# A plain first block of the MLP, small parameters as one load, and VectorE's share of the convolutions in a three-layer hybrid kernel

## The chip, the cores and the metric

The kernel runs on one core of a Trainium2 chip. The metric is the device time of one execution in microseconds (us); a lower time is better. Before the change the median of three runs is 1737.26 us (1736.63 to 1739.16).

The core's engines are TensorE (PE in the rows, its weight loads PEld), VectorE (DVE), ScalarE (ACT), GpSimd (POOL) and SyncE (SP), which issues the DMAs. Each works through its own queue in order.

## The reference

Input: x of 512 tokens by 1024, float32. Two layers of a first block and one layer of a second run one after the other.

```python
for l in range(2):                       # first block
    p = x @ w_in[l]
    y_a, y_b, y_c = mla(...), mlstm(...), ssd(...)   # ssd: 5-tap convolution over 768 channels, silu, scan
    x = layernorm(2 ** 0.5 * x + concat(y_a, y_b, y_c) @ w_out[l])
    x = layernorm(2 ** 0.5 * x + moe(x))             # 16 experts, 2 per token
h = rmsnorm(x, norm_mix_w)               # second block
x = x + concat(gated_delta_net(h), rg_lru(h)) @ w_out_2
m = rmsnorm(x, norm_mlp_w)
u = relu(m @ w_ff1)                      # 1024 x 4096
x = x + (u * u) @ w_ff2                  # 4096 x 1024
return rmsnorm(x, final_norm_w)
```

## The kernel before

**Numbers.** Every matrix product of weights and activations is made of three TensorE products: an operand is split into a high part (a cast, line 134) and a low part (the operand less its high part, line 139), and high x high, high x low and low x high are summed (lines 124 to 126). `split` takes the engine of each part: the cast is on ScalarE, the low part on VectorE or GpSimd.

**Weights.** `plan` lists all weights as tasks in the order of their use. `pump` loads a task as soon as the ring of split weights has room: SP issues a DMA into a raw buffer (line 229), then units of 1024 columns are split, the engines taken in turn from `self.pat`. In the mixers `pat` starts as ("act", "dve") and turns to ("act", "pool") behind the projection "C" of the gates (line 520), so from the convolutions on GpSimd makes the low parts. A raw buffer is loaded again when its last split has read it. The order on each engine is laid down by a planner when the kernel is built: it goes by program order and by modelled times, so that an instruction may be pulled ahead of earlier ones of its queue.

**Small parameters.** `params` (line 2007) makes one tile for each of 8, 9 or 6 groups of columns and issues one DMA for each (line 2014). The tiles have one buffer each, so a group for the next layer is loaded when the last reader of that group is done. `params_done` halves the convolution's weights (line 2018).

**The start** (`run`). SP issues four loads of x (already transposed), two of the weights "C", the parameters, then the first convolution weights into the buffers of "C". ScalarE and VectorE split x and weights, the projection "C" runs over four token tiles, and its evacuation (lines 506 to 515) has steps on VectorE and on ScalarE; two PSUM banks take turns.

**The convolutions** (`ssd_conv`, line 580). Three tasks of two features each: 24 matmuls of 512 columns make one feature (128 channels by 512 tokens). The evacuation copies it with padding (ScalarE, line 592), makes the first tap with bias on VectorE (line 594), adds four taps there (line 596), takes tanh (ScalarE, line 598), multiplies (line 600); four of the features are then transposed on TensorE (line 605). Beside this VectorE works through the small steps of the gates (lines 435 to 445 and 700 to 735), and GpSimd, besides weights, through products for the scan (lines 625 and 662).

**The MLP of the second block.** The output projection of the mixer (`out_last`, line 1016) ends tile by tile of 128 tokens; `fin` (line 1884) normalizes each tile, and `mlp_in` transposes it (line 1770) and splits it. The up projection works in 8 blocks of 512 columns. Each block is a 2 x 2 product (two halves of the 1024 features, two halves of tokens, two halves of columns) done by a scheme with 7 products instead of 8 (`up`, line 1799). It needs sums of quarter weights, made by VectorE in `up_part` (lines 260 to 264), and sums of quarter activations (T1 to T4, lines 1779 to 1786). Products 0 and 1 need plain quarters only; for block 0 they are issued in `fin` at tile 2 (line 1886), from weights split early into the buffers of T3 and T4 (line 1876). `keep` (line 1803) adds two products, squares the relu and splits the result: three steps on VectorE, one on ScalarE. The down projection of a block (`down`, line 1829) makes 8 tiles of 12 matmuls of 512 columns, each added to the residual by VectorE (line 1837). Blocks run as up 0, up 1, down 0, up 2, down 1, and so on.

Of the kernel before, what the change touches and what calls it, by code (L numbers as in the profile page):

```python
# [15 lines left out]
P = 128  # L16
# [54 lines left out]
class Kernel:  # L71
# [169 lines left out]
    def by_k(u):  # L241
        u = u.rearrange("p (k n) -> p k n", k=4)
        return [u[:, k] for k in range(4)]

    def up_part(self, b, n, u):

        v = self.nc.vector
        if n == 0:
            self.quarters = []
            for j in range(2):  # L250
                raw = self.t(self.raws[self.nraw % len(self.raws)].pool, "raw", [P, 2 * UNIT])
                self.nraw += 1
                at = b * 512 + j * 256
                self.nc.sync.dma_start(raw.rearrange("p (k n) -> p k n", n=256),
                                       self.a["w_ff1_2"][0][:, at:at + 256].rearrange("(k p) n -> p k n", p=P))
                self.quarters += [raw[:, 0:UNIT], raw[:, UNIT:2 * UNIT]]
        q = self.quarters
        if n == 2:
            q.append(self.t(self.mlpp, "sw", [P, UNIT]))
            v.tensor_tensor(q[4], q[2], q[3], op=OP.add)  # L260
            v.tensor_tensor(q[2], q[0], q[2], op=OP.subtract)  # L261
            v.tensor_tensor(q[0], q[4], q[0], op=OP.subtract)  # L262
        if n == 5:
            v.tensor_tensor(q[1], q[1], q[0], op=OP.subtract)
        self.split(u, q[(0, 1, 0, 4, 2, 1, 3)[n]], "act", "pool" if n in (1, 6) else "dve")
# [220 lines left out]
    def mixer_layer(self, l):  # L486
# [30 lines left out]
        KR = self.t(me, "KR", [P, NT, 32])  # L517
        self.proj_tok(XT, (l, "C"), 312, evac_c)
        self.cT = self.hl(m, "cT", [P, 3, S])
        self.pat = [("act", "pool")]  # L520


        lp = self.log1pexp(m, "lp", FD, [P, 2, 32])
# [20 lines left out]
        r = self.pool(x, f"ml{l}", side="right")  # L544
        self.ssd_conv(l, sp, XT)
        self.mla_in(l, m, sp, XT)
        yc = self.ssd_scan(l, sp, m, Z)
        self.sctx.close()
        with ExitStack() as y:
# [30 lines left out]
    def ssd_conv(self, l, m, XT):  # L580
        nc, a = self.nc, self.a
        cw = self.par["cw"]
        BC = self.t(m, "BC", [P, 4, S])
        xtm = self.t(m, "xtm", [P, NT, 256])
        Btm = self.t(m, "Btm", [P, NT, 256])
        self.ssd_c.update(BC=BC, xtm=xtm, Btm=Btm)

        def evac(f, p):
            xp = self.t(m, "xp", [P, S + 4], bufs=2)
            nc.gpsimd.memset(xp[:, 0:2], 0.0)  # L590
            nc.gpsimd.memset(xp[:, S + 2:S + 4], 0.0)
            nc.scalar.copy(xp[:, 2:S + 2], p)
            ac = self.t(m, "ac", [P, S], bufs=2)
            nc.vector.tensor_scalar(ac, xp[:, 0:S], cw[:, f:f + 1], cw[:, 30 + f:31 + f], op0=OP.mult, op1=OP.add)
            for k in range(1, 5):
                nc.vector.scalar_tensor_tensor(ac, xp[:, k:k + S], cw[:, 6 * k + f:6 * k + f + 1], ac, op0=OP.mult, op1=OP.add)
            th = self.t(m, "th", [P, S])
            nc.scalar.activation(th, ac, AF.Tanh)
            dst = BC[:, f - 2, :] if f >= 2 else self.t(m, "xs", [P, S])
            nc.vector.scalar_tensor_tensor(dst, th, 1.0, ac, op0=OP.add, op1=OP.mult)  # L600
            if f < 4:
                to = xtm if f < 2 else Btm
                pt = self.ps("tr", [P, 4, P])
# [1152 lines left out]
        x.close()  # L1756
        return mix[0]

    def mlp_in(self, m, i, n, X, X32):


        nc, v = self.nc, self.nc.vector
        tk, half = slice(i % 2 * P, i % 2 * P + P), i // 2
        cut = lambda n: HL(X[n].h[:, :, tk], X[n].l[:, :, tk])
        ps = []
        for g in range(2):
            p = self.ps("tr", [P, 4, P])
            for j in range(4):
                f = 4 * g + j
                nc.tensor.transpose(p[:, j, :], n[:, f * P:(f + 1) * P], self.ident)  # L1770
            nc.scalar.copy(X32[g][:, :, i * P:(i + 1) * P], p)
            if not half:
                self.split(cut(("B11", "B21")[g]), p)
            ps.append(p)
        if not half:
            return
        (b11, b12), (b21, b22) = [[x[:, :, z + i % 2 * P:z + i % 2 * P + P] for z in (0, 256)] for x in X32]
        t2 = self.t(m, "u2", [P, S], bufs=2).rearrange("p (k t) -> p k t", k=4)
        v.tensor_tensor(b11, b12, b11, op=OP.subtract)
        v.tensor_tensor(t2, b22, b11, op=OP.subtract)  # L1780
        self.split(cut("T2"), t2)
        self.split(cut("T1"), b11)
        v.tensor_tensor(b12, b22, b12, op=OP.subtract)
        self.split(cut("T3"), b12)
        self.split(cut("B22"), ps[1])
        v.tensor_tensor(b21, b21, t2, op=OP.subtract)
        self.split(cut("T4"), b21)

    def up_product(self, p, w, x):
        for z in range(2):  # L1790
            for k in range(4):
                self.mm(p[:, z * 256:(z + 1) * 256], w[k][:, z * P:(z + 1) * P], x[:, k, :], start=k == 0, stop=k == 3)

    def mlp(self, m, X, R, begun, finish):

        nc, v = self.nc, self.nc.vector
        uT = {}

        def up(b):
            u_ = self.hl(m, "uT", [P, 4, S], bufs=2)  # L1800
            s1, s5, s3, _ = [t[:, z:z + S] for t in [self.t(m, "nrm", [P, D], bufs=2) for _ in range(2)] for z in (0, S)]

            def keep(f, t, x, y):

                u = self.t(m, "u2", [P, S], bufs=2)
                v.tensor_tensor(u, x, y, op=OP.add)  # L1806
                v.scalar_tensor_tensor(u, u, 0.0, u, op0=OP.max, op1=OP.mult)  # L1807
                d = HL(*(x[:, 2 * f:2 * f + 2, 256 * t:256 * t + 256] for x in (u_.h, u_.l)))
                self.split(d, u.rearrange("p (f t) -> p f t", f=2), "act")

            def product(n, x):
                p = self.ps(("mm", "tr")[n % 2], [P, S])
                self.up_product(p, self.take(("up", b, n)), X[x])
                self.done(("up", b, n))
                return p

            A, C = (product(0, "B11"), product(1, "B21")) if b else begun
            nc.scalar.copy(s1, A)
            keep(0, 0, s1, C)
            v.tensor_tensor(s1, s1, product(2, "T2"), op=OP.add)  # L1820
            nc.scalar.copy(s5, product(3, "T1"))
            v.tensor_tensor(s3, s1, product(4, "T3"), op=OP.add)
            keep(1, 1, s3, s5)
            v.tensor_tensor(s5, s1, s5, op=OP.add)
            keep(0, 1, s5, product(5, "B22"))
            keep(1, 0, s3, product(6, "T4"))
            uT[b] = u_
# [12 lines left out]
            for hf in range(2):  # L1840
                self.done(("dn", b, hf))

        up(0)
        for b in range(8):
            if b < 7:
                up(b + 1)
# [7 lines left out]
    def second(self):  # L1854
        nc, a, v = self.nc, self.a, self.nc.vector
        with ExitStack() as c:
# [14 lines left out]
            self.mlpp = rp  # L1871
            g = self.t(rp, "sw", [P, D])
            self.bcast_load(g, a["norm_mlp_w_2"][0], D)
            X, begun = {}, []

            w0 = [self.hl(rp, t, [P, UNIT]) for t in ("T3", "T4")]
            for n in range(2):
                self.up_part(0, n, w0[n])
            for t in ("B11", "B21", "B22", "T1", "T2"):
                X[t] = self.hl(rp, t, [P, 4, 256])  # L1880
            X32 = self.hl(rp, "uT", [P, 4, S], bufs=2)
            X32 = [x.bitcast(F32) for x in (X32.h, X32.l)]

            def fin(i):
                n = self.t(rp, "nrm", [P, D], bufs=2)
                if i == 2:
                    for z in range(2):
                        p = self.ps("dn", [P, S])
                        self.up_product(p, self.by_k(w0[z]), X[("B11", "B21")[z]])
                        begun.append(p)  # L1890
                    for t in ("T3", "T4"):
                        X[t] = self.hl(rp, t, [P, 4, 256])
                self.rms(rp, n, R[:, i], g, jk=n)
                self.mlp_in(rp, i, n, X, X32)
                self.dump("x3", R[:, i], i)

            self.out_last(mixT, [("out2", q) for q in (2, 3)], add, [4, 5, 6, 7, 0, 1, 2, 3], fin)
# [1 line left out]
            with ExitStack() as x1:  # L1899
# [8 lines left out]
                        nc.sync.dma_start(self.out[0, i * P:(i + 1) * P, :], o)  # L1908
                    self.dump("out", o, i)

                self.mlp(rp, X, R, begun, finish)

    def plan(self):

# [39 lines left out]
        w2 = a["w_ff2_2"][0]  # L1954

        def up(b):
            for n in range(0 if b else 2, 7):
                add(("up", b, n), "p", [], 4, 256)
                T[-1].make = lambda u, n=n: self.up_part(b, n, u)

# [46 lines left out]
    def params(self, l):  # L2007

        self.par = r = {}
        width = dict(dtb=8, al=8, sgn=256, cw=48, gcol=32, lc=32, gc=16)  # L2010
        at = 0
        for tag, n in ROWS[l]:
            r[tag] = self.t(self.ppool, "gcol" if tag == "lc" else tag, [P, width.get(tag, n)])[:, 0:n]
            self.nc.sync.dma_start(r[tag], self.a[f"small{l}"][:, at:at + n])
            at += n

    def params_done(self):
        self.nc.vector.tensor_scalar(self.par["cw"], self.par["cw"], 0.5, None, op0=OP.mult)
# [224 lines left out]
```

## Time and profile before

| what | value |
|---|---|
| three runs, median (range) | 1737.26 us (1736.63 to 1739.16) |
| the profiled execution, its own time | 1732.17 us |
| its span (first to last instruction) | 1730.3 us |
| granted TensorE clock, mean | 0.954 |
| TensorE, VectorE, ScalarE, GpSimd busy | 90%, 75%, 48%, 32% |

An engine's busy share is a mean over stages with different limits. A row of a window gives the busy time of each engine in that stretch, the number of its instructions and the granted clock (1.00 is 2.4 GHz). A timeline row gives start, duration, engine, line and operation, and in brackets the idle time before it with what ended that. A row of waits gives the total, the number of times and the longest, all for the engine and line that waited.

### The profile page before, as it was taken

To read this page: it belongs to the slowest core of one execution; us is meant where nothing else is said; L and a number is where in the kernel's file an instruction comes from. 1 tells how busy PE (TensorE), PEld (TensorE's weight loads), DVE (VectorE), ACT (ScalarE), POOL (GpSimd) and SP (SyncE) were. 2 spreads that over 40 slices of the span, in tenths; PEclk is the share of its full clock that TensorE was granted. 3 is DMA by queue.
4 is the path that set the end of the run, shared out by engine and by line. 5 is a ranking of instruction groups with operands and counts; after the bars stand their busy time and mean duration, and the time that the engine had idled before them with its cause. 6 is when DMAs were issued, how large, how long until landed. Compare 5 with 4: busy or idle time off the path is not lost. (4 is left out here: it accounts for less than half of the span.)

```text
span 1730.3 us, 29609 instructions
## 1 busy us (share of the span) xinstructions
PE 1561.6 (90%) x11539; PEld 1398.0 (81%) x11539; DVE 1298.5 (75%) x2480; ACT 827.2 (48%) x1422; POOL 561.3 (32%) x464
## 2 busy tenths in 40 slices
PE   7899999699956899997889993999799799999997
PEld 6789899698946789887878972887578698899996
DVE  6847963789957847865689977777776797777774
ACT  4354562278856344551368863555532533333331
POOL 0555332316114555334315202003411143444341
PEclk9999999899987999999989996999999899999999
DMA  5214123499945211123399964432112243333311
GB/s 183 61 59 147 64 103 115 180 363 357 396 166 204 61 59 48 50 86 131 127 346 358 373 239 170 128 98 74 38 52 75 73 127 117 98 98 98 98 62 49
DMA packets 107662, 248.02 MB, mean 143 GB/s; under 512 B 9460, under 2 KB 70776, under 8 KB 95224
## 3 DMA queue, kind: packets, MB, share of 16 engines
q1 hardware_dynamic: 101624, 225.05, 37.4%
q0 software_dynamic: 5888, 20.97, 3.8%
q8 instruction: 94, 1.54, 0.4%
q14 instruction: 56, 0.46, 0.1%
HBM read 218.21 MB, written 27.79 MB: 142 GB/s over the span
## 5 line engine op out<-in xcount | busy, mean ns | idle before, releaser
L134 ACT CAST wh<-raw 128x1024 fp32r<-128x1024 f32 (+3 forms) x375 | 377.5, 1024 | 278.4 <-PE mm L126 70.3
L139 POOL TENSOR_TENSOR wl<-raw,wh 128x1024 fp32r<-128x1024 f32 (+3 forms) x117 | 281.3, 2414 | 474.7 <-ACT wh L134 469.0
L139 DVE TENSOR_TENSOR wl<-raw,wh 128x1024 fp32r<-128x1024 f32 (+2 forms) x258 | 307.2, 1211 | 64.3 <-ACT wh L134 63.4
L124 PE MATMUL mm<-wh,actTh 128*128 128x256 f32 (+2 forms) x640 | 189.5, 297 | 22.2 <-ACT wh L134 7.9
L126 PE MATMUL mm<-wh,actTl 128*128 128x256 f32 (+2 forms) x640 | 185.7, 292 | 2.9 <-POOL actTl L139 2.4
L125 PE MATMUL mm<-wl,actTh 128*128 128x256 f32 (+2 forms) x640 | 185.9, 291 | 0.5 <-DVE wl L139 0.5
L124 PE MATMUL mm<-actTh,wh 128*128 128x512 f32 x368 | 150.5, 409 | 2.4 <-DVE FD L509 0.8
L126 PE MATMUL mm<-actTh,wl 128*128 128x512 f32 x368 | 148.0, 402 | 0.0
L125 PE MATMUL mm<-actTl,wh 128*128 128x512 f32 x368 | 148.0, 402 | 0.0
L124 PEld LDWEIGHTS mm<-wh,actTh 128*128 128x128 f32 x640 | 124.9, 195 | 25.2 <-ACT wh L134 7.9
L126 PEld LDWEIGHTS mm<-wh,actTl 128*128 128x128 f32 x640 | 123.9, 194 | 5.4 <-POOL actTl L139 3.3
L125 PEld LDWEIGHTS mm<-wl,actTh 128*128 128x128 f32 x640 | 124.8, 195 | 1.8 <-DVE wl L139 0.9
L1089 POOL DMA_INDIRECT G<-Xd,idx x32 | 77.9, 2434 | 131.1 <-DVE oh L1138 58.3
L124 PE MATMUL dn<-wh,uTh 128*128 128x512 f32 x256 | 100.9, 395 | 3.1 <-DVE R L1837 3.1
L126 PE MATMUL dn<-wh,uTl 128*128 128x512 f32 x256 | 100.4, 392 | 0.0
L125 PE MATMUL dn<-wl,uTh 128*128 128x512 f32 x256 | 100.1, 391 | 0.1
L124 PEld LDWEIGHTS mm<-actTh,wh 128*128 128x128 f32 x368 | 70.6, 192 | 17.8 <-PE mm L126 2.2
L126 PEld LDWEIGHTS mm<-actTh,wl 128*128 128x128 f32 x368 | 70.9, 193 | 14.4
L125 PEld LDWEIGHTS mm<-actTl,wh 128*128 128x128 f32 x368 | 71.0, 193 | 14.0
L124 PE MATMUL py<-wh,GTh 128*96 128x256 f32 x256 | 73.6, 287 | 1.3 <-ACT wh L134 1.3
L124 PE MATMUL pg<-wh,GTh 128*96 128x256 f32 x256 | 74.3, 290 | 0.0
L125 PE MATMUL py<-wl,GTh 128*96 128x256 f32 x256 | 72.9, 285 | 1.1 <-DVE wl L139 1.1
(781 smaller groups left out, 4308.4 us busy)
## 6 DMA issues: line engine op xcount, KB each, us to landing
raw<-in_expert_w_gate_dram SPq DMA_DIRECT2D x32, 1024.0 KB, 10.4
raw<-in_expert_w_up_dram SPq DMA_DIRECT2D x32, 1024.0 KB, 10.3
raw<-in_expert_w_down_dram SPq DMA_DIRECT2D x32, 1024.0 KB, 10.9
raw<-in_w_ff_dram SPq DMA_DIRECT2D x32, 1024.0 KB, 5.5
raw<-in_w_in_dram SPq DMA_DIRECT2D x27, 1024.0 KB, 5.4
raw<-in_w_out_dram SPq DMA_DIRECT2D x12, 1024.0 KB, 5.2
Yd<-Ye SPq DMA_DIRECT2D x32, 384.0 KB, 6.7
Yd<-zr SPq DMA_DIRECT2D x9, 512.0 KB, 6.4
```

Source lines behind the costliest of these rows:

```text
L124: mm(out, lhsT.h, rhs.h, start=start, stop=False, **kw)
L125: mm(out, lhsT.h, rhs.l, start=False, stop=False, **kw)
L126: mm(out, lhsT.l, rhs.h, start=False, stop=stop, **kw)
L134: nc.scalar.copy(dst.h, src)
L139: (nc.gpsimd if leng == "pool" else nc.vector).tensor_tensor(dst.l, src, dst.h, op=OP.subtract)
L1089: nc.gpsimd.indirect_dma_start(out=G[:n], out_offset=None, in_=self.Xd, in_offset=bass.IndirectOffsetOnAxis(ap=idx[:n], axis=0))
```

## The change

1. The first block of the MLP is computed plainly, as four products over all 1024 features (`up_plain`), from weights that are only split, never combined. B12 (features 0 to 511 of tokens 256 to 511) gets a split form, in a buffer of the raw ring. The sums T1 to T4 are made for two token tiles at once, behind the first plain product, and split behind the third and fourth; T2 and T1, T3 and T4 take the buffers of block 0's weights.
2. `params` issues one DMA into one tile.
3. `pat` turns to ("act", "pool") only behind `mla_in`, so that the low parts of weights that are loaded during the convolutions and `mla_in` are made by VectorE.
4. The first tap of the convolutions moves from VectorE to ScalarE.

```diff
+    def up_block0(self, ws):
+        for n, (q, w) in enumerate(zip(self.up_load(0), ws)):
+            self.split(w, q, "act", ("dve", "pool")[n // 2])
...
-        self.pat = [("act", "pool")]
...
         self.ssd_conv(l, sp, XT)
         self.mla_in(l, m, sp, XT)
+        self.pat = [("act", "pool")]
...
-            nc.vector.tensor_scalar(ac, xp[:, 0:S], cw[:, f:f + 1], cw[:, 30 + f:31 + f], op0=OP.mult, op1=OP.add)
+            nc.scalar.activation(ac, xp[:, 0:S], AF.Identity, scale=cw[:, f:f + 1], bias=cw[:, 30 + f:31 + f])
...
+            x = X[f"B{g + 1}{half + 1}"]
+            self.split(HL(x.h[:, :, tk], x.l[:, :, tk]), p)
             nc.scalar.copy(X32[g][:, :, i * P:(i + 1) * P], p)
...
+    def mlp_sums(self, X, X32):
+
+        v = self.nc.vector
+        (b11, b12), (b21, b22) = [[x[:, :, z:z + 256] for z in (0, 256)] for x in X32]
         v.tensor_tensor(b11, b12, b11, op=OP.subtract)
         v.tensor_tensor(b12, b22, b12, op=OP.subtract)
+        v.tensor_tensor(b22, b22, b11, op=OP.subtract)
+        v.tensor_tensor(b21, b21, b22, op=OP.subtract)
+        return dict(T1=b11, T2=b22, T3=b12, T4=b21)
...
+        def up_plain():
+
+            u_ = self.hl(m, "uT", [P, 4, S], bufs=2)
+            W = [self.by_k(w) for w in w0]
+            C, T = [], {}
+            for f, t in ((0, 0), (1, 0), (0, 1), (1, 1)):
+                p = self.ps("dn", [P, S])
+                for z in range(2):
+                    for k in range(KD):
+                        x = X[f"B{k // 4 + 1}{t + 1}"][:, k % 4]
+                        self.mm(p[:, z * 256:(z + 1) * 256], W[2 * f + k // 4][k % 4][:, z * P:(z + 1) * P], x,
+                                start=k == 0, stop=k == KD - 1)
+                C.append((f, t, p))
+                if (f, t) == (0, 0):
+                    T = self.mlp_sums(X, X32)
+                for n in {(0, 1): ("T2", "T1"), (1, 1): ("T3", "T4")}.get((f, t), ()):
+                    X[n] = self.hl(m, n, [P, 4, 256])
+                    self.split(X[n], T[n])
+            for f, t, p in C:
+                r, u = self.t(m, "nrm", [P, D], bufs=2)[:, 0:S], self.t(m, "u2", [P, S], bufs=2)
+                nc.scalar.activation(r, p, AF.Relu)
+                v.tensor_tensor(u, r, r, op=OP.mult)
+                self.split(HL(*(x[:, 2 * f:2 * f + 2, 256 * t:256 * t + 256] for x in (u_.h, u_.l))),
+                           u.rearrange("p (f t) -> p f t", f=2), "act")
+            uT[0] = u_
...
-            A, C = (product(0, "B11"), product(1, "B21")) if b else begun
+            A, C = product(0, "B11"), product(1, "B21")
...
-        up(0)
+        up_plain()
...
-            w0 = [self.hl(rp, t, [P, UNIT]) for t in ("T3", "T4")]
-            for n in range(2):
-                self.up_part(0, n, w0[n])
-            for t in ("B11", "B21", "B22", "T1", "T2"):
-                X[t] = self.hl(rp, t, [P, 4, 256])
+            w0 = [self.hl(rp, t, [P, UNIT]) for t in ("T2", "T1", "T3", "T4")]
+            self.up_block0(w0)
+            X = {t: self.hl(rp, t, [P, 4, 256]) for t in ("B11", "B21", "B22")}
+            b12 = self.t(self.raw0.pool, "raw", [P, 2 * UNIT]).bitcast(FR).rearrange("p (z k t) -> p z k t", z=2, k=4)
+            X["B12"] = HL(b12[:, 0], b12[:, 1])
...
-            for n in range(0 if b else 2, 7):
+            for n in range(7 if b else 0):
...
-        width = dict(dtb=8, al=8, sgn=256, cw=48, gcol=32, lc=32, gc=16)
+        all_ = self.t(self.ppool, "par", [P, max(sum(n for _, n in z) for z in ROWS)])
         at = 0
         for tag, n in ROWS[l]:
-            r[tag] = self.t(self.ppool, "gcol" if tag == "lc" else tag, [P, width.get(tag, n)])[:, 0:n]
-            self.nc.sync.dma_start(r[tag], self.a[f"small{l}"][:, at:at + n])
+            r[tag] = all_[:, at:at + n]
             at += n
+        self.nc.sync.dma_start(all_[:, 0:at], self.a[f"small{l}"])
```

## Rows read from the trace of the kernel before

**Rows 1.** The page, part 1: engines over the whole span

```profile
PE 1561.6 (90%) x11539; PEld 1398.0 (81%) x11539; DVE 1298.5 (75%) x2480; ACT 827.2 (48%) x1422; POOL 561.3 (32%) x464
```

**Rows 2.** Timeline of TensorE, a dense stretch and the MLP's entry

```profile
1334.08 0.28 PE L124 MATMUL mm<-wh,actTh 128*128 128x256 f32 x1
...
1342.92 0.28 PE L124 MATMUL mm<-wh,actTh 128*128 128x256 f32 x1
...
1385.01 0.58 PE L126 MATMUL tr<-T1h,wl 128*128 128x256 f32 x1 [1.00 <-DVE wl L139]
```

**Rows 3.** Windows: length; busy us of PE, PEld, DVE, ACT, POOL; clock, DMA, GB/s

```profile
20.00:24.00 4.00, 3.39 (x13) 3.39 (x14) 1.41 (x7) 0.47 (x2) 0.00 (x0) 0.58 0.06 17
36.00:92.00 56.00, 51.06 (x224) 40.92 (x223) 46.99 (x76) 21.24 (x35) 28.68 (x30) 0.94 0.20 60
557.00:612.00 55.00, 50.61 (x225) 40.86 (x225) 46.15 (x79) 19.40 (x31) 26.97 (x24) 0.97 0.29 86
1360.40:1368.00 7.60, 6.81 (x58) 6.56 (x56) 4.08 (x11) 2.87 (x5) 2.41 (x1) 1.00 0.84 257
1368.00:1400.50 32.50, 19.66 (x127) 17.97 (x128) 31.90 (x38) 17.41 (x26) 5.16 (x1) 0.74 0.23 70
1400.50:1435.20 34.70, 31.50 (x220) 28.90 (x218) 34.14 (x33) 13.02 (x17) 17.05 (x6) 1.00 0.38 121
1435.20:1718.00 282.80, 282.80 (x1716) 252.94 (x1717) 204.31 (x223) 94.41 (x110) 107.32 (x39) 1.00 0.27 86
```

**Rows 4.** Waits of TensorE from 1360 to 1440: total, times, longest

```profile
PE tr L124 <- ACT wh L134: 9.1, 2, 7.9
PE dn L124 <- DVE R L1837: 3.1, 1, 3.1
```

**Rows 5.** Waits of TensorE in the convolutions, layer 0, then layer 1

```profile
PE tr L605 <- DVE BC L600: 2.9, 1, 2.9
...
PE tr L605 <- DVE MP L725: 3.6, 1, 3.6
```

**Rows 6.** Timelines of VectorE, SP, ScalarE and TensorE at the start

```profile
7.88 2.18 DVE L139 TENSOR_TENSOR wl<-raw,wh 128x936 fp32r<-128x936 f32 x2 [0.98 <-ACT wh L134]
...
12.70 1.01 SPq L229 DMA_DIRECT2D raw<-in_w_in_dram  x2
...
17.92 1.04 ACT L134 CAST wh<-raw 128x1024 fp32r<-128x1024 f32 x1 [4.98 <-DMA raw<-in_w_in_dram]
...
20.61 0.63 PE L124 MATMUL mm<-wh,actTh 128*128 128x312 f32 x1 [2.45 <-DVE Yc L515]
```

**Rows 7.** Timeline of VectorE at the MLP's entry

```profile
1368.50 1.23 DVE L139 TENSOR_TENSOR wl<-raw,wh 128x1024 fp32r<-128x1024 f32 x1 [2.50 <-ACT wh L134]
...
1370.78 0.69 DVE L1779 TENSOR_TENSOR uTh<-uTh 128x512 f32<-128x512 f32 x1
1371.38 0.68 DVE L139 TENSOR_TENSOR B22l<-tr,B22h 128x512 fp32r<-128x512 f32 x1
...
1416.81 3.25 DVE L261 TENSOR_TENSOR raw<-raw 128x1024 f32<-128x1024 f32 x1
```

**Rows 8.** Groups of VectorE and GpSimd from 28 to 92: busy us, mean ns | idle

```profile
L596 DVE SCALAR_TENSOR_TENSOR ac<-xp,cw,ac 128x512 f32<-128x512 f32 x24 | 21.5, 895 | 0.5
L594 DVE TENSOR_SCALAR ac<-xp,cw 128x512 f32<-128x512 f32 x6 | 8.0, 1329 | 4.1 <-ACT xp L592 4.1
...
L139 POOL TENSOR_TENSOR wl<-raw,wh 128x1024 fp32r<-128x1024 f32 x8 | 19.8, 2481 | 53.6 <-ACT wh L134 53.6
```

**Rows 9.** Timeline of VectorE in the convolutions of layer 0

```profile
67.99 2.38 DVE L725 TENSOR_TENSOR MP<-XE,CS 128x8 f32<-128x8 f32 x1
...
73.75 0.54 DVE L594 TENSOR_SCALAR ac<-xp,cw 128x512 f32<-128x512 f32 x1
...
74.44 0.75 DVE L596 SCALAR_TENSOR_TENSOR ac<-xp,cw,ac 128x512 f32<-128x512 f32 x1
```

**Rows 10.** Instructions of line 2168: ns min/median/max, first and last start

```profile
L2168 ACT ACTIVATE G<-R,lnnm,lnrs x2: 1227/1238/1250, 533.0 to 537.0; 128x1024 f32<-128x1024 f32 x2
```

More of the change, by code (lines that the diff above doesn't have):

```diff
@@ L243, in by_k, with up_load @@
         return [u[:, k] for k in range(4)]
+    def up_load(self, b):
+        q = []
+        for j in range(2):
+            raw = self.t(self.raws[self.nraw % len(self.raws)].pool, "raw", [P, 2 * UNIT])
+            self.nraw += 1
+            at = b * 512 + j * 256
+            self.nc.sync.dma_start(raw.rearrange("p (k n) -> p k n", n=256),
+                                   self.a["w_ff1_2"][0][:, at:at + 256].rearrange("(k p) n -> p k n", p=P))
+            q += [raw[:, 0:UNIT], raw[:, UNIT:2 * UNIT]]
+        return q
+    def up_block0(self, ws):
+        for n, (q, w) in enumerate(zip(self.up_load(0), ws)):
+            self.split(w, q, "act", ("dve", "pool")[n // 2])
     def up_part(self, b, n, u):
@@ L248, in up_part @@
         if n == 0:
[L249 to L256, printed above, removed]
+            self.quarters = self.up_load(b)
         q = self.quarters
@@ L1757, in hybrid, with mlp_in @@
         return mix[0]
-    def mlp_in(self, m, i, n, X, X32):
-        nc, v = self.nc, self.nc.vector
+    def mlp_in(self, i, n, X, X32):
+        nc = self.nc
         tk, half = slice(i % 2 * P, i % 2 * P + P), i // 2
-        cut = lambda n: HL(X[n].h[:, :, tk], X[n].l[:, :, tk])
-        ps = []
         for g in range(2):
@@ L1770, in mlp_in @@
                 nc.tensor.transpose(p[:, j, :], n[:, f * P:(f + 1) * P], self.ident)
+            x = X[f"B{g + 1}{half + 1}"]
+            self.split(HL(x.h[:, :, tk], x.l[:, :, tk]), p)
             nc.scalar.copy(X32[g][:, :, i * P:(i + 1) * P], p)
[L1772 to L1778, printed above, removed]
+    def mlp_sums(self, X, X32):
+        v = self.nc.vector
+        (b11, b12), (b21, b22) = [[x[:, :, z:z + 256] for z in (0, 256)] for x in X32]
         v.tensor_tensor(b11, b12, b11, op=OP.subtract)
-        v.tensor_tensor(t2, b22, b11, op=OP.subtract)
-        self.split(cut("T2"), t2)
-        self.split(cut("T1"), b11)
         v.tensor_tensor(b12, b22, b12, op=OP.subtract)
[L1784 to L1787, printed above, removed]
+        v.tensor_tensor(b22, b22, b11, op=OP.subtract)
+        v.tensor_tensor(b21, b21, b22, op=OP.subtract)
+        return dict(T1=b11, T2=b22, T3=b12, T4=b21)
     def up_product(self, p, w, x):
@@ L1792, in up_product, with mlp @@
                 self.mm(p[:, z * 256:(z + 1) * 256], w[k][:, z * P:(z + 1) * P], x[:, k, :], start=k == 0, stop=k == 3)
-    def mlp(self, m, X, R, begun, finish):
+    def mlp(self, m, X, X32, w0, R, finish):
         nc, v = self.nc, self.nc.vector
         uT = {}
+        def up_plain():
[22 more added lines that the diff above has]
+            uT[0] = u_
         def up(b):
@@ L1873, in second @@
             self.bcast_load(g, a["norm_mlp_w_2"][0], D)
-            X, begun = {}, []
-            w0 = [self.hl(rp, t, [P, UNIT]) for t in ("T3", "T4")]
-            for n in range(2):
-                self.up_part(0, n, w0[n])
-            for t in ("B11", "B21", "B22", "T1", "T2"):
-                X[t] = self.hl(rp, t, [P, 4, 256])
+            w0 = [self.hl(rp, t, [P, UNIT]) for t in ("T2", "T1", "T3", "T4")]
[3 more added lines that the diff above has]
+            X["B12"] = HL(b12[:, 0], b12[:, 1])
             X32 = self.hl(rp, "uT", [P, 4, S], bufs=2)
@@ L1885, in fin @@
                 n = self.t(rp, "nrm", [P, D], bufs=2)
[L1886 to L1892, printed above, removed]
                 self.rms(rp, n, R[:, i], g, jk=n)
-                self.mlp_in(rp, i, n, X, X32)
+                self.mlp_in(i, n, X, X32)
                 self.dump("x3", R[:, i], i)
@@ L1909, in finish @@
                     self.dump("out", o, i)
-                self.mlp(rp, X, R, begun, finish)
+                self.mlp(rp, X, X32, w0, R, finish)
     def plan(self):
```

## The prediction

> **What bounds the kernel now.** I read the page first, then the windows of the stages that the change touches, then TensorE's waits in them. TensorE is busy for 90% of the span [rows 1], so only stages in which it stands still or is clocked down can give time back. Its records overlap, so I use pitches: of two matmuls in a dense stretch of 256 columns, 78 places apart (26 groups of three), the second starts 8.84 us later, 0.1133 us each [rows 2].
>
> Three places stand out. **MLP entry.** The output projection ends at 1360.4. From there to 1368 TensorE is busy for 6.8 of 7.6 us, from 1368 to 1400.5, where block 1's first product begins, for 19.7 of 32.5 us at a mean granted clock of 0.74 (between its levels of 2.4 and 1.2 GHz). VectorE is busy there for 31.9 of 32.5 and then for 34.1 of 34.7 us [rows 3]. The longest waits are 9.1 us for high parts of combined weights and 3.1 us for a residual add on VectorE [rows 4]. After 1435.2 TensorE is busy throughout, VectorE for 204 of 283 us [rows 3]: the steady blocks are bound by TensorE, the entry by VectorE's queue. **The convolutions** of both layers: VectorE 47 of 56 and 46 of 55 us, clock 0.94 and 0.97 [rows 3]; TensorE, whose queue is in order, stands 2.9 us before transposes in layer 0 and 3.6 us in layer 1 [rows 5]. **The start:** 2.45 us before a matmul whose bank waits for evacuation steps of ScalarE, and these sit behind a cast that waited 4.98 us for a weight load [rows 6].
>
> **The change, part by part.**
>
> *Plain first block.* TensorE: 192 instead of 168 matmuls of 256 columns, 24 x 0.1133 = +2.7 us. VectorE: a step of 128x1024 holds the queue for 1.14 us (two in 2.28), one of 128x512 for 0.60 [rows 7]. Removed: four weight combinations and four weight low parts of block 0, 8 x 1.14 = 9.1; for tokens 256 to 511, 8 sums and 10 low parts of half size, 18 x 0.60 = 10.8; block 0's evacuation, 3 sums and 4 x 3 steps, 15 x 0.60 = 9.0. Added: 4 sums and 4 low parts of 1024 columns, 9.1; four low parts of B12 and B22, 2.4; evacuation 4 x 2 steps, 4.8. Net -28.9 + 16.3 = -12.6 us, out of a queue that is full from 1368 to 1435.2. One more weight low part (1.1 us) comes before 1360, beside the output projection, which covers it; without that cover it costs its 1.1. GpSimd keeps its two low parts of block 0. ScalarE gets four relus and sheds casts; it is busy for 17.4 of 32.5 us [rows 3].
>
> More important is the order. Before, products 0 and 1 (48 matmuls) ran while the last tokens were normalized; the other five needed combined weights and sums, so TensorE stood still and woke at the lower clock. After, two output halves of tokens 0 to 255 (96 matmuls, 10.9 us) need plain splits alone: with 16 transposes (about 2 us) they fill TensorE from 1360.4 to 1373.5. The low parts of B12 and B22 are due then: B22's of the first of the two tokens started at 1371.4 [rows 7]. The sums move behind the first product, and product 2 of block 1 is the first to need one.
>
> TensorE's least from 1360.4 to the state that it had at 1435.2 (blocks 0 and 1 up, four tiles of the first down projection): 2 + 192 x 0.1133 + 168 x 0.1133 + 48 x 0.234 = 54.0 us, where 0.234 is what the 282.8 us after 1435.2 [rows 3] leave for 720 matmuls of 512 columns after 1008 of 256. It took 74.8, so at most 20.8 us are to be had. By VectorE's queue it is 12.6 plus the 3.1 us wait at its end, 15.7; against this I set some 2 us for inputs of the third product that come late. I take 14, nearer to the queue's figure, since VectorE is the engine without slack there. Bounds: 3 (rival A) and 18 (midway between the two limits). What would still stretch the queue: one 1.22 us step took 3.25 us while GpSimd made low parts [rows 7]; those are the down weights', and stay.
>
> Queues: SP issues the same two loads for block 0. B12 lives in a buffer of the ring that the first down weights load into, until the plain block ends, by the sum near 1386; block 0's combined weights held these buffers until about then, so it costs nothing, and if the plain block ends late the load does by as much.
>
> *Low parts of weights on VectorE in the convolutions.* Eight low parts of 2.48 us leave GpSimd in layer 0's stage [rows 8] and cost VectorE 8 x 1.14 = 9.1 us. What they cost it now stands in its own steps: 24 taps mean 0.895 us and six first taps 1.33 [rows 8], against 0.75 and 0.54 undisturbed, and a 128x8 step took 2.38 us [rows 9] while GpSimd ran low parts. Stretch: 24 x 0.15 + 6 x 0.78 = 8 us, and some 6 us in small gate steps: 14 us.
>
> *First tap on ScalarE.* Six steps per layer leave VectorE, 6 x 0.54 = 3.3 us without stretch. Identity with two column operands took 1.24 us for 1024 columns on ScalarE [rows 10], so 512 lie between 0.62 and 1.24; I take 0.8, as part of it is fixed: 4.8 us per layer on an engine busy for 21 of 56 us [rows 3], behind a copy on the same engine.
>
> The Trainium skill (VectorE: DVE Perf Modes, Mode 2×_2P) speaks against this edit: VectorE reads a one-input fp32 operand in SBUF at two elements per cycle, so a tap moved off it loses a fast step; with some 0.25 us for each of 12 chains (an estimate) the whole sum below would be 3 us smaller. The trace agrees for the undisturbed tap (0.54 us, rows 9), while its mean is 1.33 us [rows 8].
>
> VectorE's sum in the stage: 47 - 14 - 3.3 + 9.1, and 3 of the stretch back from GpSimd work that stays (the scan's products), 42 of 56 us, so it stops being late. What is late next is the chain behind a feature (copy, tap, four taps, tanh, product: 0.8 + 4 x 0.75 and three more steps of about 0.54, 5.4 us, an estimate), about as long as the 24 matmuls of the next feature (24 x 0.234 = 5.6). To be had are the wait and the clock: 2.9 + 0.06 x 56 = 6.3 us and 3.6 + 0.03 x 55 = 5.3; I take 5 and 4, as part will stay. Bounds: 6.3 and 5.3; below, -5.8 (slower) each, if no stretch goes (9.1 - 3.3).
>
> *One parameter load.* Nine small issues on SP become one. The first convolution weights were issued at 12.70, although the last reader of their buffer, the gate weights' low part, was done at 10.06 [rows 6]: 2.6 us. They end the 4.98 us wait, and so the 2.45 us, after which the clock was 0.58 for a 4 us slice [rows 3], another 1.7. I take 3, bounds 0 and 4.2. The load for the next layer moves behind the last reader of the whole tile; its readers come a layer later, so nothing waits.
>
> **Sum:** 14 + 5 + 4 + 3 = 26 us. The profiled execution took 1732.17 us (span 1730.3), 5.1 under the median of the three runs, 1737.26. Off the median: **1711 us**.
>
> **The rivals.** *A, the hole moves.* The third plain product waits for B12's and B22's low parts, queued on VectorE behind block 1's weights and combinations (9 steps, 10.3 us from 1368.5). For: these are issued first and the queue is in order; before, the first low part that TensorE wanted came at 1385 [rows 2]. Against: the combinations were mixed with the token steps even then. TensorE would stand from 1373.5 to 1385, run 96 matmuls (10.9 us, and some 4 of half clock) and start block 1 at 1400 as before; only the 3.1 us wait goes. Gain 3 + 9 + 3 = 15: 1722 us. *B, VectorE stays the bound (slower).* If its long steps in the convolutions are not GpSimd's doing, each stage grows by 5.8 us, and the MLP's queue yields A's 3 us; the start gives 3. Net 11.6 - 6 = +5.6: 1743 us. It decides once less than 2.8 us of the 14 us of stretch per stage goes (2 x 5.8 - 2 x 2.8 = 6). Against it: the long steps stand beside GpSimd's. *C, it does not do what it says:* the planner, which orders by modelled times, lays the plain products behind the transposes and pulls other work into VectorE's queue, so each stage ends as before: 1735 to 1738 us.
>
> **How the numbers follow.** Forecast 0.63, A 0.25, B 0.06, C 0.06. The range 1702 to 1728: the forecast's bounds (18 + 6.3 + 5.3 + 4.2 = 34 gives 1703, and a little for the runs' own spread) and A with weak convolutions (3 + 5 + 1 = 9 gives 1728); B and C lie outside. A change of 0.2%, 3.5 us, is about what a measurement of this kernel can tell from none. Faster: forecast and A, 0.88; same: C, 0.06; slower: B, 0.06.
>
> **What would show it.** In the changed kernel: no wait of TensorE over 2 us and a clock near 1.00 between the end of the output projection and the first down projection, a stretch some 14 us shorter; first taps on ScalarE near 0.8 us; no VectorE step of 2 us in the convolutions except beside the scan's products; the first convolution weights issued near 10 us. The prediction is wrong if TensorE still waits for low parts in the plain block (A), if VectorE's taps still mean 0.9 us (B), or if time moves in stages that the change does not touch, such as the experts.

## The result and the profile after

The changed kernel takes **1710.54 us** (median of four runs, 1709.50 to 1711.06) against 1737.93 us (1736.63 to 1739.16) for the kernel before on the same chip: ratio 0.9842, 95% interval 0.9825 to 0.9859. The forecast was 1711 us. The profiled execution of after took 1710.83 us, span 1709.0, that is 21.3 less than before's span of 1730.3; before's profiled execution was 5 us under its own median.

The page of after, part 1 (engines over the whole span), beside [rows 1]:

```profile
PE 1569.1 (92%) x11563; PEld 1402.5 (82%) x11563; DVE 1274.3 (75%) x2466; ACT 835.7 (49%) x1431; POOL 513.2 (30%) x446
```

TensorE has 24 more matmuls and is busy for 7.5 us longer, in a span that is 21.3 shorter: it stands still for 28.8 us less. VectorE lost 24 us, GpSimd 48.

Windows of after, the stretches of [rows 3] with their new times (length; busy us of PE, PEld, DVE, ACT, POOL; clock, DMA, GB/s): a slice of the start, the convolutions of layers 0 and 1, then the MLP's entry in three parts.

```profile
20.00:24.00 4.00, 4.00 (x28) 3.79 (x27) 1.77 (x22) 0.00 (x0) 0.00 (x0) 1.00 0.02 4
33.00:89.00 56.00, 56.00 (x284) 46.01 (x283) 41.73 (x85) 28.90 (x47) 13.89 (x27) 1.00 0.29 93
547.60:602.60 55.00, 55.00 (x253) 44.12 (x252) 42.29 (x89) 26.47 (x42) 7.70 (x16) 1.00 0.33 106
1353.00:1360.40 7.40, 7.40 (x65) 7.40 (x64) 5.47 (x15) 2.12 (x4) 0.00 (x0) 1.00 0.71 217
1360.40:1388.00 27.60, 27.45 (x229) 27.19 (x228) 25.92 (x25) 18.66 (x28) 4.90 (x2) 1.00 0.51 171
1388.00:1412.50 24.50, 22.50 (x143) 19.82 (x141) 24.21 (x22) 8.53 (x11) 17.60 (x5) 1.00 0.25 87
```

In all of them the granted clock is now 1.00, and TensorE stands still for more than 0.2 us only in the last. The MLP's entry, from the output projection's end to the first residual add, takes 58.8 us (1353.7 to 1412.5, where the add starts); it took 74.1 (1360.4 to 1434.5). What TensorE still waits for there, from 1340 to 1420 (total, times, longest):

```profile
PE dn L125 <- POOL wl L139: 1.7, 1, 1.7
PE dn L124 <- DVE R L1865: 1.0, 1, 1.0
```

The 9.1 us for combined weights [rows 4] are gone, and in both convolution stages no wait of TensorE is listed any more [rows 5]. The convolutions' groups from 28 to 89 (busy us, mean ns | idle), to hold against [rows 8]:

```profile
L605 DVE SCALAR_TENSOR_TENSOR ac<-xp,par,ac 128x512 f32<-128x512 f32 x24 | 18.9, 790 | 0.7
...
L139 DVE TENSOR_TENSOR wl<-raw,wh 128x1024 fp32r<-128x1024 f32 x11 | 13.4, 1217 | 7.7 <-ACT wh L134 7.7
...
L603 ACT ACTIVATE ac<-xp,par 128x512 f32<-128x512 f32 x6 | 4.9, 811 | 0.0
```

The taps mean 0.79 us instead of 0.895, and the first tap costs 0.81 us on ScalarE. At the start, SP issues the first convolution weights at 10.27 instead of 12.70 [rows 6]:

```profile
3.62 0.44 SPq L2036 DMA_DIRECT2D par<-in_small_dram  x1
10.27 2.23 SPq L229 DMA_DIRECT2D raw<-in_w_in_dram  x2
```

**Where the 21.3 us came from.** I matched TensorE's instructions of the two kernels and read the lead of after over before at each. It is 3.2 us when the start ends, grows by 7.5 in the convolutions of layer 0 (30.4 to 100.9 of before), by 5.3 in those of layer 1 (557 to 612.5) and by 14.7 from the last output projection (1350) to the end: 30.7 us. Some 9 are lost again in stages that the change does not name: about 5 in the experts of layer 0 and around them (254 to 557), 2 between 1092 and 1300, 3 between 1300 and 1350. The experiments ask which part earns what, and where the 9 went. Where a lead is given at a time, here and below, the time is that of the first profile of before. The kernels of a group ran on one chip, beside the kernel before.

### The profile page after: what moved, and what is told of

It is laid out like the page before. It is cut to its first block, busy times and chain, and to the rows that moved or that the text cites. A ratio compares the mean times of both kernels' runs of the same rounds, so it can differ in the third digit from the quotient of the medians.

```text
span 1709.0 us, 29588 instructions
## 1 busy us (share of the span) xinstructions
PE 1569.1 (92%) x11563; PEld 1402.5 (82%) x11563; DVE 1274.3 (75%) x2466; ACT 835.7 (49%) x1431; POOL 513.2 (30%) x446
## 5 line engine op out<-in xcount | busy, mean ns | idle before, releaser
L134 ACT CAST wh<-raw 128x1024 fp32r<-128x1024 f32 (+3 forms) x371 | 373.4, 1024 | 278.5 <-PE mm L125 71.7
L139 DVE TENSOR_TENSOR wl<-raw,wh 128x1024 fp32r<-128x1024 f32 (+1 forms) x273 | 327.9, 1221 | 77.2 <-ACT wh L134 76.3
L139 POOL TENSOR_TENSOR wl<-raw,wh 128x1024 fp32r<-128x1024 f32 (+2 forms) x98 | 233.8, 2397 | 375.9 <-ACT wh L134 370.4
L1098 POOL DMA_INDIRECT G<-Xd,idx x32 | 70.9, 2216 | 135.4 <-DVE oh L1147 58.2
L126 PEld LDWEIGHTS mm<-actTh,wl 128*128 128x128 f32 x368 | 69.8, 190 | 15.7
## 6 DMA issues: line engine op xcount, KB each, us to landing
raw<-in_expert_w_down_dram SPq DMA_DIRECT2D x32, 1024.0 KB, 13.4
```

The lines of the kernel that those rows point to most:

```text
L126: mm(out, lhsT.l, rhs.h, start=False, stop=stop, **kw)
L134: nc.scalar.copy(dst.h, src)
L139: (nc.gpsimd if leng == "pool" else nc.vector).tensor_tensor(dst.l, src, dst.h, op=OP.subtract)
L1098: nc.gpsimd.indirect_dma_start(out=G[:n], out_offset=None, in_=self.Xd, in_offset=bass.IndirectOffsetOnAxis(ap=idx[:n], axis=0))
```

## Experiments

### One part undone at a time

The first group undoes each of the four parts. `u_mlp` is the kernel before with parts 2 to 4; the others are the changed kernel with

```diff
# u_mlp: mlp_in, mlp, second, plan and up_part as in the kernel before
# u_pat: low parts back on GpSimd from the gates on
         self.cT = self.hl(m, "cT", [P, 3, S])
+        self.pat = [("act", "pool")]
...
         self.mla_in(l, m, sp, XT)
-        self.pat = [("act", "pool")]
# u_tap: first tap back on VectorE
-            nc.scalar.activation(ac, xp[:, 0:S], AF.Identity, scale=cw[:, f:f + 1], bias=cw[:, 30 + f:31 + f])
+            nc.vector.tensor_scalar(ac, xp[:, 0:S], cw[:, f:f + 1], cw[:, 30 + f:31 + f], op0=OP.mult, op1=OP.add)
# u_par: nine loads (params as in the kernel before)
```

> The changed kernel with the MLP's old entry (parts 2 to 4 of the change alone). By the prediction's sum 14 us of the gain come from the plain first block, so this takes 1711 + 14 = 1725 us, ratio to before 0.993, with the hole of some 12 us in TensorE's work before block 1 as in the kernel before. By the changed kernel's own trace, where the lead at matching instructions jumps from 7 to 22 us at the MLP's entry, 15 us are lost: 1726. Rival: the hole was partly made by work that the other parts shift, and then under 10 us are lost: 1720 or less.

Measured: 1723.92 us, ratio to before 0.9938 (0.9916 to 0.9959). Against the changed kernel's 0.984 to 0.985 the plain block is worth some 16 us. The hole is as it was; waits of TensorE from 1345 to 1440:

```profile
PE tr L124 <- ACT wh L134: 9.1, 2, 7.9
PE dn L124 <- DVE R L1837: 2.6, 1, 2.6
```

So the hole was the MLP's own, and the rival falls. The lead says the same: from 1350 to 1460 it grows by 1.1 us here, by 15.0 in the changed kernel.

> The changed kernel with the low parts of the convolutions' weights back on GpSimd; the first tap stays on ScalarE. If GpSimd's low parts stretch VectorE's steps (the prediction), VectorE's taps mean about 0.9 us again, GpSimd makes some 8 low parts of 2.4 us per layer, TensorE waits before transposes again, and 6 to 9 us are lost: 1717 to 1720. Rival: it is enough that the six first taps left VectorE, since they were its most stretched steps (1.33 us each, 8 us per layer): then under 2 us are lost, 1711 to 1713.

Measured: 1712.05 us, ratio 0.9874 (0.9852 to 0.9895): some 5 us lost by the ratios, between the two. Groups from 28 to 92 of this kernel:

```profile
L139 POOL TENSOR_TENSOR wl<-raw,wh 128x1024 fp32r<-128x1024 f32 x9 | 22.2, 2466 | 48.0 <-ACT wh L134 46.2 <-PE tr L614 1.8
L605 DVE SCALAR_TENSOR_TENSOR ac<-xp,par,ac 128x512 f32<-128x512 f32 x24 | 19.9, 829 | 0.4
...
L609 DVE SCALAR_TENSOR_TENSOR BC<-th,ac 128x512 f32<-128x512 f32 x4 | 5.8, 1462 | 2.2 <-ACT th L607 2.2
```

GpSimd's low parts do stretch VectorE again, now the last step of a feature (1.46 us instead of 0.68), but TensorE waits 1.4 us only. With the first tap off VectorE most of the trouble stays away.

> The changed kernel with the first tap back on VectorE; low parts stay on VectorE. If GpSimd was the cause of the stretch, the first tap means about 0.6 us here, VectorE is busy for some 45 of 56 us in the stage and still not late: 0 to 2 us lost, 1711 to 1713. By the rule that VectorE reads such a step at two elements per cycle the chain gets 0.25 us shorter for each of 12 features: 1708. Rival: VectorE is so full with the low parts that the tap brings the waits back: 4 us or more lost, 1715.

Measured: 1709.48 us, ratio 0.9856 (0.9835 to 0.9876), not to be told from the changed kernel. With low parts on VectorE the first tap means 0.70 us there, and VectorE is busy for 45.1 of 56 us without a wait of TensorE:

```profile
L603 DVE TENSOR_SCALAR ac<-xp,par 128x512 f32<-128x512 f32 x6 | 4.2, 696 | 0.9 <-ACT xp L601 0.8
```

> The changed kernel with nine separate small loads at the start. By the prediction the first convolution weights are issued near 12.7 instead of 10.3 us and TensorE stands before the gates' projection again: 3 us lost, 1714. Rival: the time at the start is taken up later by slack in the convolutions, which are no longer late: 0 to 1 us lost, 1711.

Measured: 1704.31 us, ratio 0.9829 (0.9811 to 0.9848). Neither expectation was right: with the nine loads back it is at least as fast. The start is late again (weights issued at 12.55), yet the span ends 6.6 us earlier than after's.

### Both parts of the convolutions undone, and two kernels once more

The second group tests whether low parts and tap are substitutes, and whether the odd result of `u_par` repeats. `u_both` has the diffs of `u_pat` and `u_tap` together; `mlp_pat` those of `u_tap` and `u_par`.

> The changed kernel without parts 3 and 4: low parts back on GpSimd and the first tap back on VectorE. Undone alone, the low parts cost 1.5 us at the end of the first convolutions and the tap nothing. If the two are substitutes (either takes VectorE out of the way of the transposes), undoing both costs far more than the two alone: 7 us in the first layer and 5 in the second, 12 us over the changed kernel. If they add up, under 3 us.

Measured: 1721.21 us, ratio 0.9920 (0.9907 to 0.9934), beside 1708.37 for the changed kernel in the same group: 12.8 us lost. Undone alone the parts cost some 5 and 0 us. The lead over the two convolution stages has less scatter than the ratios: it grows by 12.8 us in the changed kernel, by 10.6 in `u_pat`, 13.4 in `u_tap` and -0.4 in `u_both`. **They are substitutes:** each takes away part of the meeting of VectorE and GpSimd, and either alone nearly clears TensorE's waits. With neither, everything is as in [rows 5] and [rows 8]; TensorE's wait in layer 0 and two groups of VectorE:

```profile
PE tr L614 <- DVE BC L609: 4.4, 1, 4.4
```

```profile
L605 DVE SCALAR_TENSOR_TENSOR ac<-xp,par,ac 128x512 f32<-128x512 f32 x24 | 21.3, 886 | 0.5
L603 DVE TENSOR_SCALAR ac<-xp,par 128x512 f32<-128x512 f32 x6 | 8.0, 1328 | 4.2 <-ACT xp L601 4.2
```

> Only the plain first block and the low parts of the convolutions on VectorE; first tap on VectorE and separate small loads, as before. If the tap and the load are worth nothing once the other two are in, this is as fast as the changed kernel or up to 3 us faster: a ratio of 0.982 to 0.986. By the prediction's sum (3 us for the start) it would be 3 us slower, 0.987.

Measured: 1705.18 us (1704.12 to 1710.07), ratio 0.9834 (0.9817 to 0.9851). The plain block and the move of the low parts alone give the whole gain, here with the nine small tiles of before.

> The changed kernel once more, beside the others of this call. Ratio to before 0.984 to 0.986. It also gives a second profile of the same code: if the changed kernel's lead over the kernel before that was lost in the experts of the first layer (8.6 us at 344, 4.4 us at 569) belongs to the code, it is lost here again; if it is the spread of one execution, the lead there differs by 2 us or more.

Measured: 1708.37 us, ratio 0.9847 (0.9828 to 0.9866), span 1709.0 again. The lead over before's first profile falls from 9.8 us at 303 to 5.2 at 569: most of the loss is there again, but at other places (3.3 us between 359 and 394, where the first profile lost 1.0).

> The kernel before once more, for a second profile. If its first profiled execution (1732.17 us, 5 us under its other runs) was short in one stage, this one shows which: the stages that differ by over 1 us between the two profiles are those where the time of one execution scatters. Expected in the experts, where the profile has waits for gathers, and not in the convolutions or the MLP.

Measured: 1733.45 us, ratio 0.9981 (0.9969 to 0.9992): the same code differs by 2.6 us from itself, which its interval does not cover, so differences of under 3 us between medians decide nothing here. The profile's span is 1734.9, 4.6 longer than that of the same code before. Matched with that one it is 1.2 us behind at 28, 1.0 at 254, 2.2 at 283, 3.9 at 557, 4.9 at 612, and 3.8 at 1350. Other than expected, it is not the experts alone that scatter: the start and the convolutions of layer 1 do so by over 1 us too.

From 254 to 557 this profile falls 2.9 us behind. In the twelve profiles of changed kernels, those of the later groups with them, the lead falls there by 1.2 to 4.9 us, by 3.3 in the mean. So **most of what after lost there is that the first profile of before was short**, and not the change. Where profiles part, the granted clock often parts too. Here are the same instructions in before, again_before and after, first from 254 to 283, then from 1300 to 1320:

```profile
254.10:283.05 28.95, 27.54 (x225) 26.04 (x224) 12.88 (x34) 9.10 (x15) 0.76 (x2) 1.00 0.40 150
255.10:285.26 30.16, 28.75 (x224) 27.44 (x223) 12.88 (x34) 9.10 (x15) 0.73 (x2) 0.94 0.40 144
243.79:274.03 30.24, 28.83 (x224) 27.54 (x223) 12.90 (x34) 9.11 (x15) 0.81 (x2) 0.94 0.40 143
```

```profile
1300.32:1320.03 19.71, 16.62 (x113) 15.37 (x114) 11.81 (x36) 3.71 (x8) 3.86 (x3) 0.83 0.34 106
1304.72:1323.60 18.88, 15.97 (x114) 14.79 (x115) 11.72 (x36) 3.74 (x8) 3.87 (x3) 0.82 0.34 112
1290.35:1312.51 22.16, 19.64 (x113) 17.84 (x114) 11.80 (x36) 3.71 (x8) 3.87 (x3) 0.69 0.29 95
```

Why the clock differs from one execution to the next is not shown.

### The single load: addresses

One difference does not scatter. In the second block's projections, 32 transposes stand at fixed places between matmuls of 512 columns. First and last start of their two groups (duration ns min/median/max, then the starts) in the changed kernel:

```profile
L1407 PE MATMUL tr<-ident,qT x16: 271/272/273, 1108.5 to 1130.2; 128*128 128x128 f32 x16
...
L1407 PE MATMUL tr<-ident,kT x16: 271/272/273, 1136.6 to 1158.7; 128*128 128x128 f32 x16
```

and in `u_par`:

```profile
L1407 PE MATMUL tr<-ident,qT x16: 270/272/273, 1106.1 to 1127.4; 128*128 128x128 f32 x16
...
L1407 PE MATMUL tr<-ident,kT x16: 270/272/273, 1133.7 to 1155.6; 128*128 128x128 f32 x16
```

The same work takes 50.3 us (1108.45 to 1158.74) and 49.5 (1106.07 to 1155.57), at clock 1.00 throughout. The mean pitch of the matmuls is 0.233 and 0.229 us (the expectations below go by the medians, 0.235 and 0.230). All six profiles with one load had the first pace, all four with nine loads the second. By the tiles' sizes the single tile is smaller, so that the buffers behind it, the weights' among them, lie 160 bytes lower. The third group tests that:

```diff
-        all_ = self.t(self.ppool, "par", [P, max(sum(n for _, n in z) for z in ROWS)])
+        all_ = self.t(self.ppool, "par", [P, 648])   # pad611: 611
```

> The changed kernel with its one parameter tile widened from 603 to 648 columns, so that every buffer behind it lies at the address it had with nine tiles (160 bytes higher). Seen so far: in the six profiled kernels with one load the matmuls of 512 columns in the second block's projections start 0.235 us apart, in the four with nine loads 0.230, at the same clock, instructions and order. If the addresses do it, the pace here is 0.230, the start keeps its 22 us, and some 3 us are gained on the changed kernel: ratio to before 0.981, 1703 us where the changed kernel takes 1708. Rival: the pace follows something else in the single load (its reads, the order built around it), and then it stays 0.235 and the ratio 0.984 to 0.985.

Measured: 1704.99 us (1702.14 to 1706.67), ratio 0.9828 (0.9815 to 0.9841). The pace is that of nine loads:

```profile
L1407 PE MATMUL tr<-ident,qT x16: 270/272/273, 1105.1 to 1126.5; 128*128 128x128 f32 x16
...
L1407 PE MATMUL tr<-ident,kT x16: 270/273/273, 1132.8 to 1154.7; 128*128 128x128 f32 x16
```

49.6 us from 1105.1 to 1154.7. The instructions of every engine and their order are those of the changed kernel, so **the addresses do it**. The ratio of 0.981 was not reached: the lead over `u_par` is 2.2 us at 254, but 0.3 at 283, where this profile has the clock of 0.94 and `u_par` 1.00, and 0.3 at the end.

> The same with 611 columns: the buffers lie 32 bytes higher than in the changed kernel. If what counts is whether the weights' buffers begin on an odd or an even multiple of 32 bytes (even in the changed kernel, odd in the kernel before), the pace is 0.230 here as well and the ratio 0.981. If it is the distance to another buffer or to a larger boundary, the pace is 0.235 or a third value, and the ratio follows it.

Measured: 1710.74 us (1704.74 to 1713.38), ratio 0.9866 (0.9851 to 0.9880). The median pitch is 0.233, which looks like a third value. But the mean is 0.233 too, and the two groups take 50.3 us (1105.25 to 1155.55): this is the changed kernel's pace, and its ratio as well. So odd or even multiples of 32 bytes are not the rule. Which distance counts stays open.

### VectorE's queue at the MLP's entry

> The changed kernel with the four low parts of the token sums T1 to T4 written twice: four more VectorE steps of 1.14 us (4.6 us) behind the first products of the plain block. If VectorE's queue still sets the end of the MLP's entry (the prediction took its gain from that queue), the first residual add comes 4 to 5 us later and the time is 4 to 5 us longer: ratio 0.987. If TensorE is the bound since its hole is filled, the queue has slack: under 1.5 us lost, 0.985.

```diff
                     self.split(X[n], T[n])
+                    v.tensor_tensor(X[n].l, T[n], X[n].h, op=OP.subtract)
```

Measured: 1719.64 us (1713.64 to 1726.24), ratio 0.9914 (0.9894 to 0.9934). 4.6 us of VectorE work (four steps that hold its queue for 1.14 each) cost 11 us: from the start of the entry's last transpose (1364.7, and 1367.3 in the changed kernel) to the end of the span it takes 352.6 us instead of 341.7. The entry has no slack for more work on VectorE, and the price is more than one for one. Waits of TensorE from 1340 to 1440, the two windows of the entry and two low parts on GpSimd show why:

```profile
PE dn L125 <- POOL wl L139: 4.5, 1, 4.5
PE mm L124 <- ACT nrm L1847: 1.9, 1, 1.9
PE tr L125 <- DVE T1l L1819: 1.2, 1, 1.2
```

```profile
1361.60:1389.00 27.40, 24.00 (x185) 23.39 (x184) 27.36 (x27) 15.90 (x22) 5.50 (x3) 0.93 0.37 119
1389.00:1424.00 35.00, 30.48 (x167) 27.09 (x166) 28.46 (x28) 8.13 (x11) 17.50 (x5) 0.86 0.18 61
```

```profile
1386.27 12.61 POOL L139 TENSOR_TENSOR wl<-raw,wh 128x1024 fp32r<-128x1024 f32 x2 [13.02 <-ACT wh L134]
```

TensorE waits for VectorE and ScalarE, then for GpSimd, and the clock comes down around both pauses (0.93, 0.86). The clock's share is up to 6.8 us (an estimate, 0.07 x 27.4 + 0.14 x 35.0). GpSimd is late beside VectorE's full queue: two low parts took it 12.6 us, where one later on takes 2.4. And VectorE is late beside GpSimd: the fourth added step takes 3.39 us (from 1396.6), so that the four held the queue for some 6.7 us and not 4.6. The expectation that the first residual add comes later did not hold: it starts 42.6 us behind the last transpose (45.2 in the changed kernel), only the second comes later (54.7 and 48.1). VectorE itself stands 5.2 us for TensorE in the second window. So the run shows that added work costs much, but not that VectorE's queue alone sets the end.

In the changed kernel the same meeting is milder but there. VectorE and GpSimd of after behind 1388:

```profile
1395.81 2.88 DVE L1835 SCALAR_TENSOR_TENSOR u<-u 128x512 f32<-128x512 f32 x1
...
1404.23 0.68 DVE L1835 SCALAR_TENSOR_TENSOR u<-u 128x512 f32<-128x512 f32 x1
```

```profile
1388.89 14.86 POOL L139 TENSOR_TENSOR wl<-raw,wh 128x1024 fp32r<-128x1024 f32 x4 [13.03 <-ACT wh L134]
```

The same step takes 2.88 us beside a low part and 0.68 without; four low parts take GpSimd 3.7 us each. The Trainium skill (SBUF — State Buffer, SBUF: two separate sides) says that VectorE and GpSimd share a pair of ports as a lock that one instruction holds to its end while the other waits, and that a VectorE step with two inputs in SBUF is subject to it. The trace agrees: 2.88 lies just under one low part (2.41, at 1373.5) and one step (0.68) after another, 3.1.

So the first down weights are a place for the change's own idea:

```diff
# on pad648
-                self.set_phase("p", [raw1, raw1, self.raw0, self.raw0], [self.ring0] * 4 + [ring1] * 2, [("act", "pool")])
+                self.set_phase("p", [raw1, raw1, self.raw0, self.raw0], [self.ring0] * 4 + [ring1] * 2, [("act", "dve")])
...
+            if b == 0:
+                self.pat = [("act", "pool")]
             down(b)
```

> The kernel with 648 columns, and the low parts of the first down projection's weights on VectorE instead of GpSimd. In the changed kernel GpSimd takes 14.9 us for these four, and VectorE's steps of 128x512 beside them take up to 2.9 us instead of 0.68, some 9 us in all. If that is GpSimd's doing as in the convolutions, VectorE gains 9 and pays 4.6, TensorE's wait of 1.7 us for GpSimd goes, and 1 to 2 us are gained on the kernel with 648 columns: ratio 0.980. Rival: VectorE's queue is full here and the four steps delay the residual adds: 2 to 4 us lost, 0.983.

Measured: **1700.88 us** (1698.21 to 1705.40), ratio 0.9808 (0.9792 to 0.9823), 4.1 us under the 1704.99 of `pad648` in the same group. It beats the changed kernel too: the interval lies below that of the changed kernel beside before (0.9828 to 0.9866). Against `pad648` the intervals still touch; by the lead from 1350 to 1460, 18.2 us instead of 14.9, some 3.3 of the 4.1 us are the edit's. The whole entry is one window without a gap, and of GpSimd's low parts there only the one behind the four is left (at 1400.1 in `pad648`):

```profile
1351.80:1399.40 47.60, 47.60 (x359) 45.49 (x359) 46.25 (x47) 26.36 (x37) 7.40 (x3) 1.00 0.43 141
```

```profile
1395.39 2.44 POOL L139 TENSOR_TENSOR wl<-raw,wh 128x1024 fp32r<-128x1024 f32 x1 [28.48 <-DVE wl L139]
```

VectorE takes four more steps and still ends earlier, because its other steps keep their 0.68 us, but for one of 2.52 beside this low part.

## Why the prediction was right, and where only its total was

*Plain first block: 14 us predicted, 14.7 by the lead and some 16 by `u_mlp`.* Right, and for the reason given: the figure was taken from VectorE's queue (15.7), not from TensorE's limit (20.8). VectorE is still busy for 24.2 of 24.5 us in the entry's last part, and relieving it there (`pad_dn0`) shortens the entry again. The 2 us set against it for inputs of the third product were not needed; no wait of rival A is in the trace.

*Convolutions: 5 and 4 us predicted, 7.5 and 5.3 measured,* the first outside its bound of 6.3, the second at its bound of 5.3. The step that failed is "to be had are the wait and the clock": it took the longest wait alone (2.9 and 3.6 us). TensorE's idle time in the windows of [rows 3] was 56 - 51.06 = 4.9 and 55 - 50.61 = 4.4 us; with the clock's 3.4 and 1.65 that makes 8.3 and 6.0. With the better addresses just that is gained: 8.3 in layer 0 (62.2 instead of 70.5 us in `u_par` and `pad648`, 62.9 in the changed kernel) and 6.0 in layer 1. VectorE's sum was too high: 42 us were predicted for the work of 36 to 92, and the same work of TensorE (32.94 to 81.00 of after) has 38.3; the 41.7 us in the 56 shown above hold more work. GpSimd's part in the long steps, on which rival B hung, was right: B falls with `u_both` against `u_tap`, 0.9920 and 0.9856.

*First tap on ScalarE.* Its price was right (0.8 us, 0.811 measured), but the prediction gave one sum for two edits and did not see that the second is worth nothing once the first is in. Undone, it changed no more than the runs can tell, in either direction (`u_tap`, `mlp_pat`). What the prediction set against this edit, a sum 3 us smaller, did not show: no wait of TensorE for the chain behind a feature is left.

*One parameter load: 3 us predicted, 3.2 in the lead at the start, none in the time.* At 28 the ten profiles with one load lead by 3.0 to 4.0 us, the other three with nine by -1.2 to 1.5. The load was costed as an issue on SP only. That it also moves every buffer behind it, and that matmuls have another pace at other addresses, no step considered. It costs about 0.8 us in layer 0's convolutions, 0.7 in layer 1's and 1.4 between 1092 and 1207, and with these the start's gain is about gone. Nor does `pad648`, which has the better addresses, beat `u_par` by the ratio (0.9828 and 0.9829); there the scatter from 254 to 283 took the start's lead. "Nothing waits" was wrong as well, but cost nothing that shows: ScalarE stands 4.2 us for the third load before line 1470, at 727.3 of after, while TensorE's lead stays at 10.3 to 10.5 us from 720 to 740.

*The sum.* 26 us were predicted and 27.4 measured by the medians. That the total came out closer than its terms is in part luck: the convolutions gave some 4 us more, and the addresses and the scatter took them. The prediction said that it would be wrong if time moved in stages such as the experts; some did. From 254 to 557 it is scatter: after lost 4.9 us, the second profile of before 2.9, all changed kernels 3.3 in the mean. From 1092 to 1300 the kernels at the slower pace lose 1.5 to 2.3 us, those at the faster one, the second profile of before among them, 0.8 to 1.0. Between 1300 and 1350 after lost 3.3, most of it up to 1320 at the clock of 0.69; the other changed kernels lie between a gain of 0.6 and a loss of 2.9, and no cause is shown.

## What to carry to other kernels

Before two engines are blamed or relieved, look whether their long steps stand beside each other: VectorE's step of 0.68 us took 2.88 beside a low part on GpSimd, and doing that low part on the busier engine itself (1.14 us of its queue) was the cheaper way in three places. To price a hole of TensorE, take the window's idle time and clock, not the longest wait in the list. When an edit changes a buffer's size, compare the pace of matmuls in stages that it does not touch, and give the old size back as a test. Take a second profile of the kernel before: stages of untouched code differed by 1 to 3 us between two executions of it.

## What the runs showed of the hardware that was not expected

Moving buffers by 160 bytes, with the same instructions in the same order and a clock of 1.00, changed the mean pitch of 512-column matmuls from 0.233 to 0.229 us (50.3 to 49.5 us for the same 201 matmuls and 32 transposes); moving them by 32 bytes left it at 0.233. Work of 4.6 us on a full VectorE queue (some 6.7 beside GpSimd's low parts) cost 11 us, up to 6.8 of them by the clock that fell around TensorE's pauses. Two edits that answer to the same collision can each look small when undone alone: 5 and 0 us by the ratios (2.2 and -0.6 by the lead), against 12.8 together (13.2 by the lead). Two profiles of one kernel differed by 2.9 us in a stretch of 303 us.
